# A hybrid HGRN2 and Hyena layer: even and odd filter spectra added by transfers, the filter network's chain kept together, h modulated by ScalarE

## The chip, the core and the metric

The kernel runs on one core of a Trainium2 chip. The core has a matrix engine (TensorE, PE in the profile), a vector engine (VectorE, DVE), a scalar engine (ScalarE, ACT), a general engine (GpSimd, POOL) and a queue engine (SyncE, SP), each with its own in-order stream of instructions, and 16 DMA engines that all queues share. SP, ACT and POOL can issue transfers; the issuing engine's stream stands still while an issue waits for its conditions. The metric is the device time of one execution in microseconds (us). Fast memory on the core is SBUF (128 partitions), PSUM is where PE writes (banks of 128 x 512 f32), DRAM is the chip's main memory.

## The reference, cut to what matters

One layer over 128 context tokens and 512 latent tokens, 640 in all, width 1024: an adaLN modulation, one wide projection, an HGRN2 branch and a Hyena branch, a mix, a norm, a SwiGLU part and a norm. The change touches two things at its start.

The modulation of the input:

```
mod = (silu(cond) @ ada_w + ada_b)        # shift1, scale1, gate1, ...
h = x * (1.0 + scale1) + shift1
proj = h @ w_in
```

And the implicit filters of the long convolution, which depend on weights alone:

```
h = sin(freq[0] * (z @ w1 + b1))
h = sin(freq[1] * (h @ w2 + b2))
h = sin(freq[2] * (h @ w3 + b3))
h = h @ w4                                # 64 -> 2 x 1024 (forward, backward)
h = h.reshape(L, 2, D_B) * window[:, None, :]
kern = concatenate([h_fwd, 0, flip(h_bwd[1:])])
K = rfft(kern, n=2 * L);  U = rfft(u, n=2 * L)
y = irfft(U * K, n=2 * L)[:, :L] + u * skip
```

## The kernel before, in words

The program has one long first stage, in function `start`, and then the projection, the branches and the rest. A plan (`PLAN`, a string of tokens) sets in which order the first stage's steps are written; a scheduler then places every instruction on its engine by what is ready and by that order, so that neighbours on an engine are not always neighbours in the plan.

The steps that the change and the prediction speak of:

- **The filter network** (`filter_mlp`, L493 to L511). Three layers on all 640 positions, two halves of 320 side by side. PE multiplies (L496, L501, L507), then DVE does four steps (add and scale L480, round L482, subtract L483, clamp L484) and ACT the sine (L171). The result goes to `hf_hi`, `hf_lo`, a high and a low part in a rounded f32 format: every large product of this kernel is three products, high by high, high by low and low by high.
- **Filter chunks** `cc` = 0 to 3, 256 of the 1024 channels each. `kern_load` (token L) loads the last weights `w4` and the window `win`; `kern_a` (A) forms sums and differences of the weights on DVE (`wsd`, L535), splits them (`whi`, `whl`), multiplies (`ks`, L544 and L545), multiplies by the window on DVE (`af`, two buffers) and splits again (`abh` by a cast, `abl` by a subtraction on DVE or POOL). An `af` buffer is free when both parts are there. Two `win` buffers exist: the load of window 2 waits for the last `af` of chunk 0, that of window 3 for the last `af` of chunk 1.
- **The chunks' spectra**, `kern_b` (B). With tables `kth`, `ktl`, loaded and split by `ktab` (tokens k0 to k2), PE makes the products `kp` (L573) and `k` (L586): for two groups `kt` an even and an odd part. ACT copies the even part out of PSUM (`ev`), and DVE makes `ko` = odd + even and even - odd (L602, L603, recorded under L182). `kern_store` (W) writes `ko` to the DRAM tensor `kd`, issued by ACT. `kd` is read much later, in `spectrum`, by loads on SP.
- **x and h.** Tokens x and T load a tile of 128 tokens and transpose it on PE (L458), ACT and DVE copy it to `xT`. Tokens D and M load 1 MB pieces of `ada_w` (`araw`, eight pieces in this stage) on SP, multiply them (L407), copy (`md`, L418), transpose (`adaT`, L431) and add into `modT`. Token h (`make_h`, L463) makes h for one of eight groups of 128 columns: a multiply-add in place on `xT` for 128 and 512 tokens, on ACT or on DVE by the string `HMOD` (L469), then a cast to `hTh` and a subtraction to `hTl`.
- **The value projection** (token V). Two units of 120 products (`v`, L715) read h and weights `raw`, loaded on SP (L350) and split into `wh` by ACT (L358) and `wl`. The first products of the next stage are `ma` (L675).

Small helpers record most of these: L182 is every two-operand operation, L185 every copy or cast by a string of engine letters (`COPIES`), L171 every ACT function. PSUM has three banks for `mm` tiles and five that all of `ks`, `kp`, `k` and the x transposes share.

Of the kernel before, what the change touches and what calls it, by code (L numbers as in the profile page):

```python
# [118 lines left out]
PLAN = """x0 k0 L0 k1 x4 k2 p mlp t L1 T0 x3 T4 A0 x2 D0 T2 A1 x1 L2 B0 M0 T1 D2 A2 M2 T3 h0 L3 B1 D1 A3 h1 B2 M1 D3 h2 h3 M3 h4 W2 W0 h5 h6 h7 W1 q V0 e0 B3 g0 W3 V1 m w0 e2 10 20 g1 50 11 60 g2 70 21 30 40 w1 w2 61 51 52 12 71 Q8 62 22 g3 w3 13 41 g4 53 72 Q9 42 31 63 w4 g5 23 14 w5 73 Z4 Q10 43 32 g6 w6 64 24 15 54 74 Q11 33 65 25 44 16 26 55 75 Q12 Z5 g7 34 w7 66 45 56 17 76 Q13 35 67 46 g8 27 57 w8 18 77 Z6 Q14 g9 g10 36 w9 28 19 68 37 29 58 78 Q15 69 47 59 w10 79 Q16 38 110 210 Z7 g11 610 49 111 510 39 48 w11 211 g12 611 112 w12 212 710 Q17 g13 511 711 Q18 410 113 w13 311 612 Z8 310 411 512 712 Q19 513 213 613 412 713 312 413 313 Z9"""  # L119
HMOD = "SVSSVSSS"  # L120
# [43 lines left out]
def body(tc, I, O):  # L164
# [5 lines left out]
    def act(out, in_, func, bias=0.0, scale=1.0):  # L170
        r = S.activation(out, in_, func, bias=bias, scale=scale)  # L171
# [282 lines left out]
    def x_transpose(t, xs):  # L454
        for q in range(2):
            ps = sc_bank(f"xT{t}_{q}")
            for k in range(4):
                PE.transpose(ps[:, k * P:k * P + P], xs[:, (4 * q + k) * P:(4 * q + k + 1) * P], ident)  # L458
# [34 lines left out]
    def filter_mlp():  # L493
# [5 lines left out]
        for hf in range(2):  # L499
            cs = slice(hf * ORD, hf * ORD + ORD)  # L500
            PE.matmul(ps[cs, 0:HT], w2[cs], h1[cs], start=True, stop=True)  # L501
# [98 lines left out]

    def order_after(ins, prev):
        if prev is not None:  # L602
            tc.add_manual_dep(  # L603
                ins.ins, prev.ins.name,
                mybir.DependencyInfo(mybir.DependencyClass.NoSync, mybir.DependencyReason.DATA),
                reason="issue order")
# [123 lines left out]
    def start():  # L730
# [43 lines left out]
        for tok in PLAN.split():  # L774
            if tok == "mlp":
                if HP:
                    with tc.high_priority():
                        filter_mlp()
                else:
                    filter_mlp()  # L780
# [1026 lines left out]
```

## Time and profile before

| | us |
|---|---|
| median of 3 runs | 1414.06 (1412.3 to 1414.61) |
| the profiled execution, its own time | 1413.15 |
| the profiled execution, span from first to last instruction | 1411.4 |
| PE busy | 1371.7 (97%) |
| DVE, ACT, POOL busy | 995.7, 620.0, 63.4 |
| PE busy in the first 150 | 125.56 |
| first `ks` product, first `kp`, first `ma` start at | 23.26, 36.99, 115.52 |

The profile is one execution. A row of a timeline gives start, length, engine, source line, operation, what is written and read, shape, how many, and in brackets how long the engine was idle just before and who ended that. A row of the groups gives busy us and mean ns, and idle time before with its releasers. Neighbouring matmuls overlap, so that a row is longer than the step from its start to the next one's. `SPq` and `ACTq` are rows of issued transfers.

### The profile page before, as it was taken

How to read it: one execution, taken by the hardware profiler on the slowest of the kernel's cores; microseconds unless marked ns; L12 is line 12 of the kernel's file. 1: busy time of each engine (PE TensorE's matmuls, PEld its weight loads, DVE VectorE, ACT ScalarE, POOL GpSimd, SP SyncE). 2: the span in 40 equal slices, each digit the busy share in tenths (PEclk: the TensorE clock that was granted, in tenths of full speed). 3: DMA queues.
4: the chain of work that ended last, by engine and by line, in shares of the span. 5: the costliest groups of instructions: out<-in, count | busy, mean ns of one | idle time of the engine just before them, and what ended most of it. 6: DMA issues, size and time to landing. Idle time of an engine off the chain costs nothing. (4 is left out here: it accounts for less than half of the span.)

```text
span 1411.4 us, 23424 instructions
## 1 busy us (share of the span) xinstructions
PE 1371.7 (97%) x9513; PEld 1290.8 (91%) x9513; DVE 995.7 (71%) x1752; ACT 620.0 (44%) x1010; POOL 63.4 (4%) x56
## 2 busy tenths in 40 slices
PE   4999999999999999999999999999999999999997
PEld 2689889899999999999999999988999999998886
DVE  6886786656889743648888786568987776765426
ACT  3555554442323211536655655227654443542121
POOL 4230000010000000000000000000000000000003
PEclk9999999999999999999999999999999999999999
DMA  7944666675323373432222223551653213267211
GB/s 246 334 139 146 208 207 195 184 232 193 101 83 102 90 246 131 135 115 82 81 86 77 64 63 109 174 196 75 169 162 102 81 59 118 89 201 263 75 60 75
DMA packets 198855, 195.63 MB, mean 139 GB/s; under 512 B 7581, under 2 KB 155773, under 8 KB 197980
## 3 DMA queue, kind: packets, MB, share of 16 engines
q1 hardware_dynamic: 194860, 179.75, 40.5%
q0 software_dynamic: 2160, 9.15, 1.8%
q10 hardware_dynamic: 1728, 5.24, 0.9%
q8 instruction: 74, 1.21, 0.4%
q14 instruction: 33, 0.27, 0.1%
HBM read 162.91 MB, written 31.21 MB: 138 GB/s over the span
## 5 line engine op out<-in xcount | busy, mean ns | idle before, releaser
L182 DVE TENSOR_TENSOR wl<-raw,wh 128x1024 fp32r<-128x1024 f32 x96 | 117.3, 1223 | 133.1 <-ACT wh L358 132.3
L358 ACT CAST wh<-raw 128x1024 fp32r<-128x1024 f32 x90 | 94.1, 1049 | 220.9 <-PE pb L612 41.0
L1431 PE MATMUL fo<-wh,act 128*128 128x512 f32 (+1 forms) x440 | 130.7, 380 | 0.0
L1431 PEld LDWEIGHTS fo<-wh,act 128*128 128x128 f32 x440 | 81.2, 188 | 16.0
L1431 PE MATMUL fo<-wl,act 128*128 128x512 f32 (+1 forms) x220 | 83.4, 379 | 0.0
L612 PE MATMUL hy<-hTh,wh 128*128 128x320 f32 x256 | 79.6, 311 | 0.0
L612 PE MATMUL hy<-hTh,wl 128*128 128x320 f32 x256 | 79.1, 309 | 0.0
L612 PE MATMUL hy<-hTl,wh 128*128 128x320 f32 x256 | 79.1, 309 | 0.0
L612 PE MATMUL f<-hTh,wh 128*128 128x320 f32 x224 | 70.7, 316 | 0.0
L612 PE MATMUL f<-hTl,wh 128*128 128x320 f32 x224 | 69.7, 311 | 0.0
L612 PE MATMUL f<-hTh,wl 128*128 128x320 f32 x224 | 69.2, 309 | 0.0
L182 POOL TENSOR_TENSOR y<-y,gb 128x512 f32<-128x512 f32 x8 | 11.6, 1454 | 888.4 <-ACT y L171 888.1
L1431 PEld LDWEIGHTS fo<-wl,act 128*128 128x128 f32 x220 | 41.3, 188 | 7.9
L612 PEld LDWEIGHTS hy<-hTh,wh 128*128 128x128 f32 x256 | 48.1, 188 | 0.0
L612 PEld LDWEIGHTS hy<-hTl,wh 128*128 128x128 f32 x256 | 48.1, 188 | 0.0
L612 PEld LDWEIGHTS hy<-hTh,wl 128*128 128x128 f32 x256 | 48.0, 188 | 0.0
L171 ACT ACT_TABLE_LOAD x36 | 46.2, 1283 | 1.4 <-PEq L1791 0.7
L715 PE MATMUL v<-wl,hTh 128*128 128x256 f32 x160 | 45.0, 286 | 1.6 <-DVE wl L182 1.6
L715 PE MATMUL v<-wh,hTl 128*128 128x256 f32 x160 | 45.1, 284 | 0.1
L715 PE MATMUL v<-wh,hTh 128*128 128x256 f32 x160 | 44.9, 285 | 0.0
L612 PEld LDWEIGHTS f<-hTl,wh 128*128 128x128 f32 x224 | 42.2, 188 | 0.0
L612 PEld LDWEIGHTS f<-hTh,wh 128*128 128x128 f32 x224 | 42.1, 188 | 0.0
(2293 smaller groups left out, 4699.6 us busy)
## 6 DMA issues: line engine op xcount, KB each, us to landing
raw<-in_w_in SPq DMA_DIRECT2D x52, 512.0 KB, 3.8
araw<-in_ada_w SPq DMA_DIRECT2D x20, 1024.0 KB, 6.5
rm<-in_w_in SPq DMA_DIRECT2D x28, 512.0 KB, 4.6
rp<-in_ffn_w_in SPq DMA_DIRECT2D x24, 512.0 KB, 5.4
raw<-in_ffn_w_out SPq DMA_DIRECT2D x22, 512.0 KB, 4.6
rf<-in_ffn_w_in SPq DMA_DIRECT2D x18, 512.0 KB, 5.2
sd<-my SPq DMA_DIRECT2D x28, 320.0 KB, 2.3
kk<-kd SPq DMA_DIRECT2D x20, 256.0 KB, 2.7
```

What stands on the lines that cost most here:

```text
L171: r = S.activation(out, in_, func, bias=bias, scale=scale)
L182: return (eng or V).tensor_tensor(out=out, in0=a, in1=b, op=op)
L358: (V.tensor_copy if HIE[i] == "V" else S.copy)(hi, raw)
L612: r = PE.matmul(ps[:, 0:HT], w[a][:, k, :], x[b][:, k, c0:c0 + HT], start=k == 0 and i == 0, stop=k == kt - 1 and i == 2)
L715: PE.matmul(ps[:, (t - t0) * 256:(t - t0) * 256 + 256], hT[b][:, k, t * P:t * P + P], w[a][:, k % 4, :], start=k == 0 and i == 0, stop=k = ...
L1431: PE.matmul(ps, x(t, b, k0 + kk), w[a][:, kk, :], start=first and kk == 0 and i == 0, stop=last and kk == nk - 1 and i == 2)
```

## The change

The plan's first tokens, before:

```
x0 k0 L0 k1 x4 k2 p mlp t L1 T0 x3 T4 A0 x2 D0 T2 A1 x1 L2 B0 M0 T1 D2 A2 M2 T3 h0 L3 B1 D1 A3 h1
B2 M1 D3 h2 h3 M3 h4 W2 W0 h5 h6 h7 W1 q V0 e0 B3 g0 W3 V1 m w0 e2 10 20 g1 50 11 60 g2 70 ...
```

And now:

```
x0 L0 x4 p mlp k0 k1 k2 t L1 x3 T4 A0 x2 D0 T2 A1 x1 L2 B0 W0 M0 T1 D2 A2 M2 T3 h0 L3 B1 W1 D1 A3 h1
B2 W2 M1 D3 h2 h3 M3 h4 h5 h6 h7 q V0 e0 B3 W3 g0 V1 m w0 e2 10 20 g1 50 11 60 K0 g2 70 ...
```

K1, K2 and K3 follow between tokens of the next stage. So the tables (k) are loaded after the network's tokens, T0 has moved into the network, each store (W) stands behind its spectrum (B), and K is new. The diff without the plan:

```diff
-HMOD = "SVSSVSSS"
+HMOD = "SSSSSSSS"
...
-COPIES = {... 'k': 'VSS', ...}
+COPIES = {...}
...
+EVB = 2
...
-    kd = dr.tile([4, P, NB, 2, 256], F32, name="kd")
+    kd = [dr.tile([P, NB, 2, 256], F32, name=f"kd{cc}") for cc in range(4)]
+    evd = [dr.tile([P, 2, 2, 256], F32, name=f"evd{cc}") for cc in range(4)]
...
-    skp_all = sp.tile([1, D], F32, name="skp_all")
...
-        G.dma_start(skp_all, I["hy_skip"])
...
-    def x_transpose(t, xs):
+    def x_transpose(t, xs, after=None):
...
+                if q == 0 and k == 0:
+                    order_after(x, after)
...
-        V.tensor_scalar(a, a, HALF, -HALF, ALU.min, ALU.max)
-        act(a, a, AF.Sin, scale=-TWO_PI)
+        net["clamp", nm] = V.tensor_scalar(a, a, HALF, -HALF, ALU.min, ALU.max)
+        net["sin", nm] = act(a, a, AF.Sin, scale=-TWO_PI)
...
-            PE.matmul(ps[cs, 0:HT], w2[cs], h1[cs], start=True, stop=True)
+            net["f2"] = PE.matmul(ps[cs, 0:HT], w2[cs], h1[cs], start=True, stop=True)
         h2 = sin_layer(ps[:, 0:HT], 1, "2")
+        x_transpose(0, xs0, net["f2"])
...
-        cpy("k", i, kth[:, cs], raw)
+        order_after(S.copy(kth[:, cs], raw), net["sin", "2"])
...
-        return w4, win, skp_all[:, c0:c0 + 256]
+        skp = sp.tile([1, 256], F32, tag="skp", bufs=2, name=f"skp{cc}")
+        SY.dma_start(skp, I["hy_skip"][:, c0:c0 + 256])
+        return w4, win, skp
...
-        tt(wsd[:, 0], w4[:, 0], w4[:, 1], ALU.add)
-        tt(wsd[:, 1], w4[:, 0], w4[:, 1], ALU.subtract)
+        for i, op in enumerate((ALU.add, ALU.subtract)):
+            x = tt(wsd[:, i], w4[:, 0], w4[:, 1], op)
+            if cc == 0:
+                order_after(x, net["clamp", "2"])
...
-            ev = sp.tile([P, 2, 256], F32, tag="ev", bufs=1, name=f"ev{cc}_{kt}")
-            cpy("o", 3 * cc + 1 + kt, ev, pk[0].rearrange("p (x n) -> p x n", x=2))
-            od = pk[1].rearrange("p (x n) -> p x n", x=2)
+            ev, od = (x.rearrange("p (x n) -> p x n", x=2) for x in pk)
+            e = sp.tile([P, 2, 256], F32, tag="ev", bufs=EVB, name=f"ev{cc}_{kt}")
+            cpy("o", 3 * cc + 1 + kt, e, ev)
             t = kout(2, kt)
-            tt(t[:, 0], od, ev, ALU.add)
-            tt(t[:, 1], ev, od, ALU.subtract)
-            out.append((t, 2 * kt, 2))
+            S.copy(t[:, 0], od)
+            S.mul(t[:, 1], od, -1.0)
+            out.append((t, 2 * kt, 2, e))
...
-        for t, f, n in out:
-            KQ.dma_start(kd[cc, :, f:f + n], t)
+        for t, f, n, e in out:
+            KQ.dma_start(kd[cc][:, f:f + n], t)
+            if n == 2:
+                KQ.dma_start(evd[cc][:, f // 2], e)
+
+    def kern_add(cc):
+        for kt in range(2):
+            for i in range(2):
+                G.dma_start(kd[cc][:, 2 * kt + i], evd[cc][:, kt], accum_op=ALU.add)
```

`order_after(a, b)` only fixes that `a` stands behind `b` on their engine; it waits for nothing more. The odd part is copied twice by ACT, once with its sign turned, and stored to `kd`; the even part is stored to a DRAM tensor of its own (`evd`); then POOL issues transfers (`kern_add`) that add `evd` into `kd` in DRAM, four for each chunk. An adding transfer waits until both stores it needs have landed.

The network, DVE between its second and third layer. Before (`kth` and `whl` are the table's and the weights' casts, `wsd` the weights' sums):

```order
L484 TENSOR_SCALAR sa_175<-sa_175 128x320
L185 CAST kth<-kt_141 128x768
L182 TENSOR_TENSOR wsd_259<-w_0_145 128x256 x2
L480 TENSOR_SCALAR sa_185<-f_182,fpar 128x320
L482 TENSOR_SCALAR sk_187<-sa_185 128x320
L185 CAST whl_264<-whi_262 64x512
L483 SCALAR_TENSOR_TENSOR sa_185<-sk_187,sa_185 128x320
L182 TENSOR_TENSOR whl_264<-wsd_259,whi_262 64x512
L484 TENSOR_SCALAR sa_185<-sa_185 128x320
```

Now:

```order
L493 TENSOR_SCALAR sa_170<-sa_170 128x320
L489 TENSOR_SCALAR sa_180<-f_177,fpar 128x320
L491 TENSOR_SCALAR sk_182<-sa_180 128x320
L492 SCALAR_TENSOR_TENSOR sa_180<-sk_182,sa_180 128x320
L493 TENSOR_SCALAR sa_180<-sa_180 128x320
L189 TENSOR_TENSOR wsd_268<-w_0_147 128x256 x2
```

The second layer's four steps follow the first layer's with nothing in between; the casts and the sums stand behind them. On ACT, from the first layer's sine to the third's, now (`sa_180` is the second layer's sine, `sa_204` the third's first half, `xT` the copies of two x tiles):

```order
L192 COPY xT_137<-xT_1_194 128x2x128
L171 ACTIVATE sa_180<-sa_180 128x320
L192 COPY xT_138<-xT_1_194 128x2x128
L192 CAST whi_271<-wsd_268 128x512
L527 CAST kth<-kt_224 128x768
L192 COPY xT_135<-xT_0_254 128x2x128
L192 COPY xT_136<-xT_0_254 128x2x128
L527 CAST kth<-kt_228 128x768
L192 COPY xT_137<-xT_1_261 128x2x128
L171 ACTIVATE sa_204<-sa_204 128x320
```

All three casts of the table are ACT's now, and two of them stand ahead of the third layer's sine.

The turn to the value projection. ACT before (`md` is the copy of the last ada product, `wh` the casts of the first `raw` tiles):

```order
L418 COPY md_861<-ada_852 128x512
L599 DMA kd<-ko_1_679 128x1024
L358 CAST wh_919<-raw_917 128x1024
L358 CAST wh_925<-raw_923 128x1024
L358 CAST wh_931<-raw_929 128x1024
L185 CAST abh_0_701<-af_0_697 128x512
```

ACT now, and PE now from the end of chunk 1's products:

```order
L613 DMA kd_67<-ko_1_697 128x1024
L363 CAST wh_938<-raw_936 128x1024
L363 CAST wh_944<-raw_942 128x1024
L423 COPY md_889<-ada_880 128x512
L192 CAST whl_714<-whi_712 64x512
L363 CAST wh_950<-raw_948 128x1024
```

```order
L600 MATMUL k_1_1_670<-abh_4_398,ktl 128x256
L412 MATMUL ada_880<-araw_0_866,scT 32x512 x4
L412 MATMUL ada_880<-araw_1_868,scT 32x512 x4
L436 MATMUL adaT_891<-cst,md_889 128x128 x4
L558 MATMUL ks_0_717<-whl_714,hf_hi 128x512
L559 MATMUL ks_0_717<-whl_714,hf_lo 128x512
```

The copy `md` and chunk 3's `whl` now stand behind two casts of `raw`, and PE's next rows read `md` and `whl`. Before, `ks` of chunk 3 (which stood between the two halves of this ada product) and the products of chunk 2 came before any row that needs `raw`.

POOL's queue now, from the first to the third chunk's `abl` (`kd<-evd` are the adding transfers):

```order
L189 TENSOR_TENSOR abl_1_372<-af_1_367,abh_1_371 128x512
L620 DMA kd_66<-evd_70 128x512 x2
L189 TENSOR_TENSOR abl_3_390<-af_3_387,abh_3_389 128x512
L189 TENSOR_TENSOR abl_4_399<-af_4_396,abh_4_398 128x512
L620 DMA kd_66<-evd_70 128x512 x2
L189 TENSOR_TENSOR abl_0_541<-af_0_536,abh_0_540 128x512
```

Before, the four `abl` rows followed each other.

More of the change, by code (lines that the diff above doesn't have):

```diff
@@ L116, in _constants @@
     return {k: np.ascontiguousarray(v) for k, v in c.items()}
[L119 to L120 removed]
+PLAN = """x0 L0 x4 p mlp k0 k1 k2 t L1 x3 T4 A0 x2 D0 T2 A1 x1 L2 B0 W0 M0 T1 D2 A2 M2 T3 h0 L3 B1 W1 D1 A3 h1 B2 W2 M1 D3 h2 h3 M3 h4 h5 h6 h7 q V0 e0 B3 W3 g0 V1 m w0 e2 10 20 g1 50 11 60 K0 g2 70 21 30 40 w1 w2 61 51 52 12 71 K1 Q8 62 22 g3 w3 13 41 g4 53 72 Q9 K2 42 31 63 w4 g5 23 14 w5 73 Z4 Q10 K3 43 32 g6 w6 64 24 15 54 74 Q11 33 65 25 44 16 26 55 75 Q12 Z5 g7 34 w7 66 45 56 17 76 Q13 35 67 46 g8 27 57 w8 18 77 Z6 Q14 g9 g10 36 w9 28 19 68 37 29 58 78 Q15 69 47 59 w10 79 Q16 38 110 210 Z7 g11 610 49 111 510 39 48 w11 211 g12 611 112 w12 212 710 Q17 g13 511 711 Q18 410 113 w13 311 612 Z8 310 411 512 712 Q19 513 213 613 412 713 312 413 313 Z9"""
+HMOD = "SSSSSSSS"
 HSUB = "GVVVVGVG"
@@ L141 @@
 PSA2 = dict(mm=("mm", 4), sc=("x", 4), o=("x", 4), tr=("x", 4))
-COPIES = {'x': 'SSVSSSSSSS', 'h': 'SSSSSSSV', 'm': 'SV', 'k': 'VSS', 'w': 'SVVS', 'v': 'VSSS', 'a': 'SSSSSSSSSVVSSSSSSSSS', 'o': 'SSSSSSSSVSSS'}
+COPIES = {'x': 'SSVSSSSSSS', 'h': 'SSSSSSSV', 'm': 'SV', 'w': 'SVVS', 'v': 'VSSS', 'a': 'SSSSSSSSSVVSSSSSSSSS', 'o': 'SSSSSSSSVSSS'}
 ASUB = "GVVVGVGVGGGGVGVGVVVG"
 KSUB = "GGG"
-HP = False
+EVB = 2
 PS0 = {'mm': ('mm', 3), 'sc': ('x', 5), 'o': ('x', 5), 'tr': ('x', 5)}
@@ L179, in act, with order_after @@
         return r
+    def order_after(ins, prev):
+        if prev is not None:
+            tc.add_manual_dep(
+                ins.ins, prev.ins.name,
+                mybir.DependencyInfo(mybir.DependencyClass.NoSync, mybir.DependencyReason.DATA),
+                reason="issue order")
     def tt(out, a, b, op, eng=None):
@@ L457, in x_transpose @@
             for k in range(4):
-                PE.transpose(ps[:, k * P:k * P + P], xs[:, (4 * q + k) * P:(4 * q + k + 1) * P], ident)
+                x = PE.transpose(ps[:, k * P:k * P + P], xs[:, (4 * q + k) * P:(4 * q + k + 1) * P], ident)
+                if q == 0 and k == 0:
+                    order_after(x, after)
             for i in range(2):
@@ L475, in make_h @@
         tt(hTl[:, k, :], xT[:, k, :], f32(hTh[:, k, :]), ALU.subtract, G if HSUB[k] == "G" else V)
+    net = {}
     def sin_layer(psrc, i, nm):
@@ L491, in body, with filter_mlp @@
     ktl = sp.tile([P, 2304], F32R, name="ktl")
-    def filter_mlp():
+    def filter_mlp(xs0):
         ps = sc_bank("f1")
@@ L576, in kern_b @@
         cpy("o", 3 * cc, t[:, 0], pk.rearrange("p (x n) -> p x n", x=2))
-        out = [(t, 4, 1)]
+        out = [(t, 4, 1, None)]
         for kt in range(2):
@@ L587, in kern_b @@
                                       start=i == 0 and j2 == 0, stop=i == 2 and j2 == 1)
-            ev = sp.tile([P, 2, 256], F32, tag="ev", bufs=1, name=f"ev{cc}_{kt}")
-            cpy("o", 3 * cc + 1 + kt, ev, pk[0].rearrange("p (x n) -> p x n", x=2))
-            od = pk[1].rearrange("p (x n) -> p x n", x=2)
+            ev, od = (x.rearrange("p (x n) -> p x n", x=2) for x in pk)
+            e = sp.tile([P, 2, 256], F32, tag="ev", bufs=EVB, name=f"ev{cc}_{kt}")
+            cpy("o", 3 * cc + 1 + kt, e, ev)
             t = kout(2, kt)
-            tt(t[:, 0], od, ev, ALU.add)
-            tt(t[:, 1], ev, od, ALU.subtract)
-            out.append((t, 2 * kt, 2))
+            S.copy(t[:, 0], od)
+            S.mul(t[:, 1], od, -1.0)
+            out.append((t, 2 * kt, 2, e))
         return out
     def kern_store(cc, out):
-        for t, f, n in out:
-            KQ.dma_start(kd[cc, :, f:f + n], t)
[L601 to L606, printed above, removed]
+        for t, f, n, e in out:
[6 more added lines that the diff above has]
+                G.dma_start(kd[cc][:, 2 * kt + i], evd[cc][:, kt], accum_op=ALU.add)
     def dense_fm(w, x, half, ps, kt=KT, after=None):
@@ L746, in step @@
                 kern_store(i, ab[i])
+            elif op == "K":
+                kern_add(i)
             elif op == "k":
@@ L775, in start @@
             if tok == "mlp":
[L776 to L780, printed above, removed]
+                filter_mlp(xs[0])
                 continue
@@ L972, in spectrum @@
         kk = q.tile([P, 2, 256], F32, tag="kk", bufs=2, name=f"kk{cc}_{f}")
-        SY.dma_start(kk, kd[cc, :, (0, 2, 1, 3, 4)[f]])
+        SY.dma_start(kk, kd[cc][:, (0, 2, 1, 3, 4)[f]])
         ps = sc_bank(f"fw{cc}_{f}")
```

## The prediction

> **What bounds the kernel now.** I read the windows by stage first, to see where TensorE (PE) is idle at all.
>
> ```profile
> 0.00:150.00 150.00, 125.56 (x854) 105.75 (x855) 114.99 (x213) 77.97 (x140) 39.10 (x37) 0.98 0.65 216
> 150.00:300.00 150.00, 148.73 (x1003) 135.08 (x1002) 105.05 (x174) 75.39 (x131) 2.72 (x1) 1.00 0.66 204
> 300.00:1380.00 1080.00, 1075.61 (x7543) 1031.32 (x7542) 751.72 (x1308) 461.94 (x731) 9.97 (x10) 1.00 0.38 120
> ```
>
> The first number after the length is PE's busy time. It idles 24.4 us in the first 150, 1.3 in the next 150 and 4.4 in the 1080 after. The order of the work differs only in the first 170 us or so, so whatever is won or lost by the first matmul of the stage that follows (`ma`) reaches the end nearly whole. Six rows of PE's timeline come next (start, length, engine, line, operation, and in brackets the idle time ahead of it and who ended that).
>
> ```profile
> 8.57 1.33 PE L501 MATMUL f<-sa,w 64*64 64x320 f32 x4 [2.46 <-ACT sa L171]
> 17.12 1.44 PE L507 MATMUL f<-sa,w 64*128 64x320 f32 x4 [7.22 <-ACT sa L171]
> ...
> 23.26 0.73 PE L544 MATMUL ks<-whl,hf_hi 128*128 128x512 f32 x2 [1.44 <-ACT hf_hi L185]
> ...
> 36.99 0.39 PE L573 MATMUL kp<-abh,kth 128*128 128x256 f32 x1
> ...
> 44.01 0.60 PE L458 MATMUL xT<-cst,xs 128*128 128x128 f32 x4
> ...
> 115.52 0.31 PE L675 MATMUL ma<-hTh,wmg0h 128*128 128x320 f32 x1
> ```
>
> The longest wait is the filter network's third layer (L507). Between its second and third layer stand VectorE (DVE) and ScalarE (ACT) rows that wait for loads:
>
> ```profile
> 10.45 0.56 DVE L185 CAST kth<-kt 128x768 fp32r<-128x768 f32 x1 [2.43 <-DMA kt<-in_kt]
> 12.76 0.76 DVE L182 TENSOR_TENSOR wsd<-w 128x256 f32<-128x256 f32 x2 [1.75 <-DMA w<-in_filt_w]
> 13.44 0.60 DVE L480 TENSOR_SCALAR sa<-f,fpar 128x320 f32<-128x320 f32 x1
> ...
> 15.87 0.83 ACT L185 CAST kth<-kt 128x768 fp32r<-128x768 f32 x1 [1.70 <-DMA kt<-in_kt]
> 16.61 0.47 ACT L171 ACTIVATE sa<-sa 128x320 f32<-128x320 f32 x1
> 19.07 0.83 ACT L185 CAST kth<-kt 128x768 fp32r<-128x768 f32 x1 [2.00 <-DMA kt<-in_kt]
> ```
>
> A second limit runs beside it, the loads on SP's queue. Filter window 3 waits for DVE's last `af` of the chunk before; eight 1 MB loads (`araw`) and the first weights (`raw`) stand behind it.
>
> ```profile
> 46.69 0.55 SPq L527 DMA_DIRECT2D win<-in_win  x1
> 47.36 10.54 SPq L398 DMA_DIRECT2D araw<-in_ada_w  x4
> 57.98 3.62 SPq L350 DMA_DIRECT2D raw<-in_w_in  x3
> ...
> araw<-in_ada_w SPq DMA_DIRECT2D x1, 1024.0 KB, 7.6
> ...
> 32.50:35.00 2.50, 2.50 (x10) 1.83 (x7) 2.01 (x4) 1.22 (x2) 1.15 (x1) 0.53 0.13 37
> 45.00:47.50 2.50, 2.48 (x17) 1.14 (x10) 2.50 (x5) 1.17 (x3) 0.65 (x1) 1.00 0.10 40
> 60.00:70.00 10.00, 10.00 (x70) 6.27 (x65) 7.96 (x20) 7.16 (x12) 2.60 (x2) 1.00 1.07 376
> ...
> 68.38 2.95 ACT L358 CAST wh<-raw 128x1024 fp32r<-128x1024 f32 x3
> ```
>
> In windows the last two numbers are the DMA engines' busy share and GB/s. Outside the two holes at 32.5 and 45 they are full (1.07, 376 GB/s), and just when they have delivered `raw`, ScalarE casts it (68.38) and PE turns to the value projection. So this stage has two clocks that tie, PE and the transfers. A shorter start pays only if the transfers follow. The last 1 MB load is issued by 57.98 - 0.55 = 57.4 (0.55 as the issue above) and lands 7.6 later, at 65.0; two `raw` loads of 0.52 MB at 376 GB/s, 1.4 us each, then make the second `raw` land at about **67.8**. No row gives that landing itself; the second cast's start bounds it at 69.4 (68.38 and one cast of 1.0).
>
> **Part 1, the network's chain.** Layer 2 ends on PE at 8.57 + 1.33 = 9.90. DVE's four steps on it began at 13.44, 3.5 later than they could; now they follow at once. The lengths that this part needs (busy us, mean ns):
>
> ```profile
> L482 DVE TENSOR_SCALAR sk<-sa 128x320 f32<-128x320 f32 x4 | 1.3, 323 | 0.1
> L483 DVE SCALAR_TENSOR_TENSOR sa<-sk,sa 128x320 f32<-128x320 f32 x4 | 2.0, 488 | 0.1
> L185 ACT COPY xT<-xT 128x256 f32<-128x256 f32 x18 | 5.6, 379 | 1.4 <-PE xT L458 1.4
> L185 ACT CAST hf_hi<-sa 128x320 fp32r<-128x320 f32 x1 | 0.5, 461 | 0.0
> L185 ACT CAST hTh<-xT 128x640 fp32r<-128x640 f32 x7 | 5.1, 731 | 2.0 <-DVE xT L469 2.0
> ```
>
> 0.60 + 0.32 + 0.49, and the clamp at 0.33 like the step before: 1.75, so 11.7; the sine (0.47) ends at 12.2 and layer 3 starts there, 4.9 earlier. The eight transposes of x_prompt now ahead of layer 3 lie in the gap; their input landed by 10.45, since it is issued ahead of the kt load that DVE got then. But behind layer 3 ScalarE's order is now kt cast, two copies, kt cast, copy, third sine. The kt loads move behind the first window and one x tile; the last of them still lands near 19.07, as the same bytes are ahead of it, and the second one load earlier (0.39 MB at 376 GB/s, 1.0), at 18.0. Cast 0.83, copy 0.38, sine 0.47, third kt cast 0.83 and the cast of the network's output 0.46 add 3.0: `ks` starts near **21.0**, 2.3 ahead of 23.26. Were ScalarE held by nothing, layer 3's end at 13.7 and two passes of DVE's steps would give 18; were the loads 2 us later than I take them, nothing is gained: -5 to 0. Then the first chunk's chain no longer has four copies of x ahead of its casts on ScalarE, and one ada product moves behind `kp`: I take `kp` at 32.5, 4.5 ahead, and the end of the products behind it at 40.5, 3.5 ahead of 44.01, because ScalarE now empties more of the banks between them.
>
> **Part 2, the adding transfers.** Removed from DVE, added to ScalarE:
>
> ```profile
> L182 DVE TENSOR_TENSOR ko<-k,ev 128x512 f32<-128x512 f32 x8 | 5.5, 682 | 0.1
> L182 DVE TENSOR_TENSOR ko<-ev,k 128x512 f32<-128x512 f32 x8 | 5.4, 678 | 0.0
> L469 DVE TENSOR_SCALAR xT<-xT,modT 128x512 f32<-128x512 f32 x2 | 4.1, 2026 | 0.0
> L185 ACT COPY ev<-k 128x512 f32<-128x512 f32 x7 | 4.1, 589 | 4.7 <-DVE ko L182 3.9 <-PE k L586 0.8
> L171 ACT ACTIVATE xT<-xT,modT 128x512 f32<-128x512 f32 x6 | 4.9, 810 | 0.0
> L171 ACT ACTIVATE xT<-xT,modT 128x128 f32<-128x128 f32 x6 | 3.0, 498 | 0.0
> ```
>
> DVE loses 5.5 + 5.4 + 4.1 = 15.0 us. ScalarE gains 16 x 0.59 = 9.4, and for two modulations 2 x (0.81 + 0.50) = 2.6; with eight more stores to issue, about 15. DVE's relief is off PE's path until `af` of chunk 1, and that is what frees window 3: I take its issue at **43.7**, 3.0 ahead of 46.69 (it follows the 3.5 above).
>
> What the DMA engines get in their place is charged here. Per chunk: two stores of 0.26 MB and four adding transfers of 0.26 MB. No row shows an adding transfer. The nearest rows are the transfers GpSimd issues, and the old stores:
>
> ```profile
> q0 software_dynamic: 2160, 9.15, 1.8%
> ...
> kd<-ko ACTq DMA_DIRECT2D x6, 512.0 KB, 3.7
> ```
>
> 1.8% of 1411.4 us is 25.4 us of all 16 engines for 9.15 MB, 360 GB/s: a copy's rate. I take an adding transfer as one copy, 0.7 us, being nearest to that row; the bounds are 0 (it runs beside loads that do not fill the engines) and 3 copies, 2.1 us (two reads and a write one after the other). The Trainium skill, *DMA: Bandwidth & Descriptors*, "Rules for kernel authors", says that an accumulate reads its destination and writes it later, and that queues share the same 16 engines; by it the estimate is the upper bound, rival B below. No row here shows it either way.
>
> Between window 3's issue and the second `raw`'s landing the old kernel stores 1.3 MB (two parts of 0.52, one of 0.26). Now it is 0.26 + 0.52 of chunk 0, 1.05 of its adding transfers, and 0.52 + 0.52 + 0.26 + about half of the late 0.52: 3.4. That is 2.1 MB more, 5.6 us at 376 GB/s. So the second `raw` lands at 67.8 - 3.0 + 5.6 = **70.4**.
>
> **Part 3, what waits for it.** In the new order ScalarE casts two `raw` tiles, then copies `md`, then `whl`; PE's next matmuls (`adaT`, then `ks` of chunk 3) wait for just these. In the old kernel `md` came before the casts and PE had `ks` and `k` work. So `ks` of chunk 3 starts at 70.4 + 1.0 + 0.6 + 0.6 = 72.6 (a cast, then the md and whl copies, as long as the `ev` copy); PE idles before it some 10 us, which is where its lead is spent. From there to `ma` stand 10 `ks` and 348 products:
>
> ```profile
> 65.08 0.40 PE L544 MATMUL ks<-whl,hf_hi 128*128 128x512 f32 x1
> 65.31 0.39 PE L545 MATMUL ks<-whl,hf_lo 128*128 128x512 f32 x1
> ...
> 101.13 0.28 PE L715 MATMUL v<-wh,hTh 128*128 128x256 f32 x1
> 115.40 0.28 PE L715 MATMUL v<-wl,hTh 128*128 128x256 f32 x1
> ```
>
> 0.23 each, and 120 from 101.13 to 115.52, 0.12 each: 2.3 + 41.8 + 0.2 of transposes = 44.3. `ma` starts at 116.9 for 115.52: **1.4 us later**. The modulations on ScalarE cost nothing in this sum: from there its work to the last h part is seven pairs of 1.3, six casts of 0.73 and some 11 copies of 0.6, about 20 us, to 93, and the 176 products after the last part (21.1) could end at 114.
>
> GpSimd's queue now waits twice per chunk for a store to land (3.7) and then issues; behind it stand the `abl` of the next chunk, for whose slot DVE's next `af` waits. While `k` products are left on PE this is hidden; uncovered it is up to 3.7 a time.
>
> **Sum.** The profiled execution took 1413.15 for a span of 1411.4. With +1.4: 1414.5, against a median of 1414.06, which the profiled one is 0.9 below. About 0.2% (2.8 us) is what a measurement here can tell from no change; so this is no change.
>
> **The rivals.**
> A, *the lead survives* (faster). If the loads fill the two holes (2.2 us each lost at 32.5 and 45) and adding transfers cost the loads nothing, `raw` comes by 65 and PE keeps its lead at `kp`, 4.5 to 6: 1407 to 1409. For: DVE's waits and the holes both hang on the same late chain. Against: 60 to 70 is full already.
> B, *the transfers decide* (slower). At 3 copies each, chunk 0's four add 4 x 1.4 = 5.6 and half of chunk 1's 1 to 2: `raw` at 77.5, `ma` at 124, +8.5: 1421.5. It decides from about 1.5 copies on (+2.8). For: 1.07 busy. Against: queue 0's 360 GB/s.
> C, *ScalarE or GpSimd's queue decides* (slower). ScalarE was busy 7.2 of 10 us from 60 to 70 and gets 15 us more by 110; two uncovered waits of 3.7 on GpSimd's queue, or layer 3 no earlier because of the kt casts (+2.6): +3 to +6, 1416.5 to 1419. For: its order is fixed and holds loads. Against: DVE's 15 us gone.
> That the sums stay on the path (the change does nothing of what it says) I rule out: the 16 DVE rows are gone from the order.
>
> **How the numbers follow.** Forecast 0.42, A 0.30, B 0.18, C 0.10. The forecast's own range, 1411.3 to 1417, is the "same" case. Range 1406.5 to 1418.5: it takes in A, C and half of the way to B. Faster 0.30; same 0.42; slower 0.28.
>
> **What would show it.** Layer 3 at 12 to 13 and `ks` at 20 to 21 show part 1; `kp` at 32 to 33 and window 3 near 44 the lead; an idle PE between 60 and 72 released by `adaT` or `whl`, and `raw` casts waiting for a DMA, show part 3; `ma` near 116.9 shows the sum. A full DMA row up to 77 is B; PE with no gap near 65 and `ma` at 110 is A. I am wrong if PE's gap there is released by GpSimd or VectorE, or if `ma` moves and the end does not.

## The result

The changed kernel takes 1429.40 us (median of 4 runs, 1428.70 to 1430.36) against 1413.29 for the kernel before: a ratio of 1.0118, 95% interval 1.0105 to 1.0130. It is 16 us slower, where no change had been forecast. The profiled execution took 1429.06 us for a span of 1427.2.

PE's windows of the changed kernel by stage (start and end, length, busy us of PE, PEld, DVE, ACT and POOL, granted clock, DMA share, GB/s):

```profile
0.00:150.00 150.00, 115.89 (x743) 97.47 (x744) 98.33 (x180) 82.27 (x149) 51.63 (x52) 0.87 0.82 239
150.00:300.00 150.00, 148.78 (x1003) 135.28 (x1002) 105.15 (x168) 76.22 (x134) 0.00 (x0) 1.00 0.63 195
300.00:1380.00 1080.00, 1075.66 (x7571) 1032.43 (x7570) 757.48 (x1323) 464.93 (x738) 12.78 (x11) 1.00 0.39 124
```

Nearly all of it lies in the first 150 us: PE is busy 115.89 there for 125.56, and 111 matmuls fewer are done. Over the whole span PE idles 48.7 us for 39.7 and is busy 1378.5 for 1371.7, so 9.0 us are idle time and 6.8 are the same work done more slowly: the mean clock of the stage is 0.87 for 0.98.

PE's timeline of the changed kernel at the places that the prediction spoke of (start and us, then the idle time ahead and what ended it):

```profile
12.71 0.88 PE L517 MATMUL f<-sa,w 64*128 64x320 f32 x4 [0.83 <-ACT sa L171]
20.57 1.22 PE L558 MATMUL ks<-whl,hf_hi 128*128 128x512 f32 x2 [3.50 <-ACT hf_hi L192]
30.98 0.77 PE L558 MATMUL ks<-whl,hf_hi 128*128 128x512 f32 x1 [2.85 <-DVE whl L189]
36.85 0.39 PE L587 MATMUL kp<-abh,kth 128*128 128x256 f32 x1
54.79 0.66 PE L463 MATMUL xT<-cst,xs 128*128 128x128 f32 x4 [2.22 <-DVE af L189]
67.62 1.94 PE L412 MATMUL ada<-araw,scT 128*32 128x512 f32 x8 [3.61 <-DMA araw<-in_ada_w]
79.01 0.66 PE L436 MATMUL adaT<-cst,md 128*128 128x128 f32 x4 [3.24 <-ACT md L423]
89.09 0.58 PE L600 MATMUL k<-abh,kth 128*128 128x256 f32 x1 [4.39 <-ACT ko_p L192]
```

The group of the first `ma` (min/median/max ns of one, first and last start):

```profile
L689 PE MATMUL ma<-hTh,wmg0h x4: 309/309/312, 133.4 to 134.7; 128*128 128x320 f32 x4
```

The network's third layer starts 4.4 us earlier than before and `ks` 2.7, but `kp` no earlier (36.85 for 36.99). From there PE falls behind in the four waits of the last rows, for VectorE, for a load and twice for ScalarE, and `ma` starts 17.9 us late. VectorE's timeline of the same execution:

```profile
21.85 2.05 DVE L189 TENSOR_TENSOR wsd<-w 128x256 f32<-128x256 f32 x1
24.22 0.67 DVE L189 TENSOR_TENSOR af<-ks,win 128x512 f32<-128x512 f32 x1
82.08 5.75 DVE L565 SCALAR_TENSOR_TENSOR af<-af,skp 1x256 f32<-1x256 f32 x1
```

ScalarE's, at the second cast of `raw` and ahead of PE's last wait:

```profile
77.42 1.04 ACT L363 CAST wh<-raw 128x1024 fp32r<-128x1024 f32 x1 [0.39 <-DMA raw<-in_w_in]
87.94 0.62 ACT L192 CAST abh<-af 128x512 fp32r<-128x512 f32 x1 [2.74 <-DVE af L565]
```

GpSimd's:

```profile
17.19 6.42 POOL L189 TENSOR_TENSOR ktl<-kt,kth 128x768 fp32r<-128x768 f32 x3 [8.30 <-ACT kth L527]
50.95 1.78 POOL L620 DMA_DIRECT2D kd<-evd  x2 [5.05 <-issue]
81.72 2.68 POOL L189 TENSOR_TENSOR wl<-raw,wh 128x1024 fp32r<-128x1024 f32 x1
84.64 2.90 POOL L189 TENSOR_TENSOR wl<-raw,wh 128x1024 fp32r<-128x1024 f32 x1
```

SP's waits (us in total, times, longest):

```profile
SPq L403 <- DMA kd<-ko_p: 8.1, 1, 8.1
```

SP's issues at that place (timelines), two 1 MB loads in one row before, and the second of the same two now:

```profile
33.76 1.17 SPq L398 DMA_DIRECT2D araw<-in_ada_w  x2
42.52 0.37 SPq L403 DMA_DIRECT2D araw<-in_ada_w  x1
```

The DMA queues' part of the page (packets, MB, share of 16 engines' span):

```profile
q0 software_dynamic: 4432, 13.34, 3.7%
```

Four things to read there. VectorE has rows several times their length (2.05 us for the 0.41 of the same row at 26.57, 5.75 for the 0.41 at 88.83) just while GpSimd has rows of its own. GpSimd stands still for 5.05 us ahead of the first adding transfers; the row names no releaser (`issue`), the rows of later ones name a store `kd<-ko`. SP's queue waits 8.1 us, ahead of a 1 MB `araw` load, for a store of the kind `kd<-ko_p` to land; before, no row of SP's waits names a store to `kd`. And queue 0 takes 3.7% of 1427.2, 52.8 us of all 16 engines, for 1.8% of 1411.4, 25.4: sixteen adding transfers are 27.4 us, **1.71 each** (the shares are rounded to 0.1%, so 1.6 to 1.8).

### The profile page after: what moved, and what is told of

It is laid out like the page before. It is cut to its first block, busy times and chain, and to the rows that moved or that the text cites. A ratio compares the mean times of both kernels' runs of the same rounds, so it can differ in the third digit from the quotient of the medians.

```text
span 1427.2 us, 23471 instructions
## 1 busy us (share of the span) xinstructions
PE 1378.5 (97%) x9513; PEld 1297.9 (91%) x9513; DVE 987.8 (69%) x1731; ACT 631.6 (44%) x1031; POOL 76.0 (5%) x71
## 3 DMA queue, kind: packets, MB, share of 16 engines
q10 hardware_dynamic: 2880, 7.34, 1.3%
```

## The experiments

Each kernel ran beside the kernel before on the same chip; the ratio's 95% interval stands in brackets, and microseconds are (ratio - 1) x 1413. The diffs of e1 to e3 show only what differs in kind. e5, e10 and e14 leave the even part out of the spectra, e6 the odd part, and e12 the tables' low part.

| run | what it is | ratio | us |
|---|---|---|---|
| (the change) | | 1.0118 [1.0105, 1.0130] | +16.7 |
| e4 | h on ScalarE alone | 0.9993 [0.9984, 1.0003] | -1.0 |
| e2 | network order alone | 1.0042 [1.0027, 1.0057] | +5.9 |
| e1 | both, sums on VectorE | 1.0042 [1.0027, 1.0057] | +5.9 |
| e3 | sums by transfers alone | 1.0148 [1.0131, 1.0165] | +20.9 |
| e10 | e3 without adding transfers | 1.0059 [1.0041, 1.0078] | +8.3 |
| e5 | change without adding transfers | 1.0052 [1.0037, 1.0067] | +7.3 |
| e6 | change, plain copies for adding | 1.0085 [1.0070, 1.0100] | +12.0 |
| e7 | change, adding in one go at 130 us | 1.0171 [1.0156, 1.0186] | +24.2 |
| e11 | change, adding one by one, 130 to 300 us | 1.0145 [1.0125, 1.0166] | +20.5 |
| e8 | change, first wl on VectorE | 1.0130 [1.0115, 1.0145] | +18.4 |
| e9 | e2, chunk 2's whl early | 1.0010 [1.0001, 1.0019] | +1.4 |
| e12 | e2, no ktl | 1.0025 [1.0015, 1.0035] | +3.5 |
| e13 | change, md and whl first | 1.0151 [1.0135, 1.0166] | +21.3 |
| e14 | e5, md and whl first | 1.0067 [1.0054, 1.0081] | +9.5 |
| e15 | e9, h on ScalarE, tables early | 1.0015 [1.0006, 1.0024] | +2.1 |
| e16 | e9, h on ScalarE, ktl on VectorE | 0.9984 [0.9975, 0.9993] | -2.3 |
| e17 | e4, ktl on VectorE | 1.0018 [1.0009, 1.0027] | +2.5 |
| e18 | change with e16's two mends | 1.0128 [1.0112, 1.0143] | +18.1 |

### The three parts apart: e1, e2, e3, e4

The first theory (T) put it all on the adding transfers, its rival (N) on the network's order.

e1 is the change with

```diff
-            S.copy(t[:, 0], od)
-            S.mul(t[:, 1], od, -1.0)
-            out.append((t, 2 * kt, 2, e))
+            tt(t[:, 0], od, ev, ALU.add)
+            tt(t[:, 1], ev, od, ALU.subtract)
```

without `evd` and `kern_add`, and the stores at their old tokens.

> The change without its adding transfers: VectorE makes the even and odd sums again, the network's chain and h on ScalarE stay. Theory T (the adding transfers cost the time: each holds the 16 DMA engines 1.7 us, 27.4 us for 16 by queue 0's row, and GpSimd stands still before each pair): 1408 to 1414, ma at 110 to 115, no PE gap released by araw near 65. Theory N (the network's new order costs it: PE at half clock from 16 to 35 us, so the lead of 2.7 us at the first ks is gone at kp): 1420 or more, ma at 122 or later. If only the lead is lost and nothing else, 1413 to 1415.

e2 is e1 with the old `HMOD`:

```diff
-HMOD = "SSSSSSSS"
+HMOD = "SVSSVSSS"
```

> The network's new order alone (sums on VectorE, old split of h). If the network order is what costs the 5.4 us that stayed without adding transfers (1418.6): 1417 to 1420, with PE at half clock between 20 and 35 us and a PE gap near 50 behind VectorE. If h on ScalarE is what costs it: 1410 to 1414.

e3 is the change with the old network order and the old `HMOD`:

```diff
-        x_transpose(0, xs0, net["f2"])
-                order_after(x, net["clamp", "2"])
-        order_after(S.copy(kth[:, cs], raw), net["sin", "2"])
+        cpy("k", i, kth[:, cs], raw)
```

> The adding transfers alone on the old network order and the old split of h between VectorE and ScalarE (the skip vector in four small loads, as the change has it, since the second ev buffer needs the room). Theory T: 1426 to 1431, as slow as the whole change, with PE gaps released by araw and by a GpSimd abl. Theory N: 1413 to 1416, since the old order keeps PE's clock.

e4 is the kernel before with

```diff
-HMOD = "SVSSVSSS"
+HMOD = "SSSSSSSS"
```

> h's modulation on ScalarE alone, on the kernel before. If it costs the 5.4 us: 1417 to 1420. By the prediction it is free: 1412.5 to 1414.

h on ScalarE is free (e4), as predicted. The network's order, meant as a gain, costs 5.9 us by itself (e2, and e1 the same). The sums by transfers cost 20.9 by themselves (e3). Neither theory is whole: both parts cost, and they do not add up (26.8 apart, 16.7 together). The sums by transfers are here all that comes with them, the copies on ScalarE and the moved and additional stores too.

### Why the network's order costs: e9, e12

Behind its start, e2's PE waits longest here (its timeline):

```profile
51.19 0.77 PE L557 MATMUL ks<-whl,hf_hi 128*128 128x512 f32 x1 [4.43 <-DVE whl L189]
```

VectorE's timeline of e2 has these rows ahead of that `whl`:

```profile
47.24 0.68 DVE L189 TENSOR_TENSOR ko<-k,ev 128x512 f32<-128x512 f32 x1
47.84 1.22 DVE L192 CAST abh<-af 128x512 fp32r<-128x512 f32 x1
48.97 0.68 DVE L189 TENSOR_TENSOR ko<-ev,k 128x512 f32<-128x512 f32 x1
49.57 0.74 DVE L192 COPY xT<-xT 128x256 f32<-128x256 f32 x2
50.33 0.72 DVE L189 TENSOR_TENSOR whl<-wsd,whi 64x512 fp32r<-64x512 f32 x1
```

In the kernel before, the same `whl` stood at 43.06, ahead of the second pair of `ko` sums. e9 puts it there again:

```diff
-        cpy("w", cc, whi, wsd)
-        cpy("v", cc, whl[0:ORD], f32(whi[0:ORD]))
-        tt(whl[ORD:P], wsd[ORD:P], f32(whi[ORD:P]), ALU.subtract)
+        with (tc.high_priority() if cc == 2 else ExitStack()):
+            cpy("w", cc, whi, wsd)
+            cpy("v", cc, whl[0:ORD], f32(whi[0:ORD]))
+            tt(whl[ORD:P], wsd[ORD:P], f32(whi[ORD:P]), ALU.subtract)
```

> The network's order alone, with the cast and the subtraction that make chunk 2's whi and whl put three places earlier on VectorE, ahead of the second pair of ko sums; nothing else there moves by more than a place. Theory O (the new order costs 5.5 us because scheduling put chunk 2's whl behind these sums and two copies, so that PE waits 4.4 us at 51 and then runs its ks at half clock): 1413 to 1416, kp of chunk 1 near 54 for 58.9. Theory L (it costs because the network's lead is lost before the first kp): unchanged, 1418 to 1420.

Chunk 1's `kp` starts at 54.11 for 58.91, and the cost falls from 5.9 to 1.4 us: 4.5 us of it went with one row of VectorE's order, which the scheduler had moved when the network's rows moved. Not all of this is shown to be that row's: in the profiled executions the first `kp`, ahead of it, already comes at 35.43 for 36.53, and PE's granted clock from 20 to 35 us is 1.00 in e9 and 0.50 in e2, though nothing that the edit names lies there.

e12 takes GpSimd's three table rows out of e2:

```diff
     ktl = sp.tile([P, 2304], F32R, name="ktl")
+    G.memset(ktl.bitcast(F32), 0.0)
...
-        tt(ktl[:, cs], raw, f32(kth[:, cs]), ALU.subtract, G if KSUB[i] == "G" else V)
```

> The network's order alone, with the table's low part (ktl) set to zero ahead of everything in place of GpSimd's three subtractions (so K lacks its smallest products). If GpSimd's rows at 17 to 23.6 us hold up VectorE there (its rows of 2.0 to 2.2 us for 0.4 to 0.7) and with it eat the network's lead: no VectorE row over 1 us from 17 to 25, first af at 22 to 23 for 24.2, first kp at 34 to 35 for 36.5, and 1415 to 1418. If PE's half clock eats it: first kp at 36 to 37, 1418 to 1420.

VectorE's rows of e12 at the place where e2 and the change have the 2 us rows:

```profile
21.25 0.41 DVE L189 TENSOR_TENSOR wsd<-w 128x256 f32<-128x256 f32 x1
21.58 0.48 DVE L189 TENSOR_TENSOR hf_lo<-sa,hf_hi 64x320 fp32r<-64x320 f32 x1
22.30 0.69 DVE L189 TENSOR_TENSOR af<-ks,win 128x512 f32<-128x512 f32 x1 [0.25 <-PE ks L558]
```

`wsd` is 0.41 again, the first `af` starts at 22.30 for 23.88, the first `kp` at 34.1 for 36.5, `ma` at 117.8 for 120.3, and the time falls by 2.4 us (the two intervals overlap). So GpSimd's rows took a good part of the network's lead: the change moves the tables, and with them these rows, to 17 to 23.6 us, where VectorE needs the network's last steps. In the kernel before two of the three had ended by 18.6. How much is less sure: these are single executions, and e3 and e10, which differ in nothing up to there, have their first `kp` 1.6 us apart (34.78 and 36.38). That PE ran its first `ks` at about half its pace in the change (1.22 for two, 0.73 before) has a part that no run took apart: PE's clock from 20 to 40 us was 0.91 in e12 and 0.60 in e2; but e4, which loses nothing, had 1.22 there too.

That a lead at `ks` need not reach `kp` is shown by more than the change: in it and in e5, e6, e7, e8, e11, e13 and e14, whose edits all lie behind `kp`, the first `ks` starts anywhere from 19.54 to 23.75 and the first `kp` always from 36.35 to 37.85.

### What the adding transfers cost, and where: e5, e6, e7, e11, e10

e5 and e10 empty `kern_add` in the change and in e3:

```diff
-        for kt in range(2):
-            for i in range(2):
-                G.dma_start(kd[cc][:, 2 * kt + i], evd[cc][:, kt], accum_op=ALU.add)
+        pass
```

> The change with the sixteen adding transfers left out (so the even part is missing from K), all stores and ScalarE copies kept. Theory T: 1408 to 1414. If ScalarE's 15 us of extra work and the eight more stores cost the time instead: 1424 or more. Theory N: 1424 or more.

> The old network order with ScalarE's copies and all stores, without the sixteen adding transfers (so the even part is missing from K). If the adding transfers are all of the 19.9 us that they cost on the old order: 1412 to 1415. If the eight more stores and ScalarE's copies have a part in it: 1416 or more. Below 1411: moving the sums off VectorE is worth something if adding is free.

e6 copies in place of adding:

```diff
-                G.dma_start(kd[cc][:, 2 * kt + i], evd[cc][:, kt], accum_op=ALU.add)
+                G.dma_start(kd[cc][:, 2 * kt + i], evd[cc][:, kt])
```

> The change with the sixteen adding transfers turned into plain copies of the same bytes from the same place to the same place, with the same waits (so K's products hold the even part alone). If the adding itself is dear (1.7 us of the 16 engines by queue 0's row, against 0.7 for a copy): a good half of the 9.5 us that the adding transfers cost comes back, 1422 to 1425, and queue 0 takes 11 us less. If GpSimd's standing still and the DRAM traffic as such cost it: 1428 to 1430.

The sixteen adding transfers cost 9.3 us on the new order (16.7 - 7.3) and 12.6 on the old (20.9 - 8.3). Queue 0's row of e6:

```profile
q0 software_dynamic: 3408, 13.34, 2.6%
```

2.6% of e6's span of 1424.0 is 37.0 us, less 25.4: 0.73 for a copy of 0.26 MB, so adding takes **2.35 times** as long on the same engines (2.1 to 2.7 with the rounding of the shares). That dearness is half of the cost: 4.7 of the 9.3 us go with it, and as plain copies they still cost 4.7.

e7 and e11 move them out of the stage:

```diff
+        if "late" not in net:
+            net["late"] = G.tensor_copy(net["v"][0:1, 4, 0:1], net["v"][0:1, 4, 0:1])
...
+                order_after(G.dma_start(...), net["late"])
```

> The change with all sixteen adding transfers behind the second value unit's store (a one-element copy on GpSimd that waits for it), at about 130 us, where GpSimd has nothing to do until 300. Theory T, with the place deciding (in the first stage they hold up araw and raw, later nothing is near its limit: DMA share 0.63 from 150 to 300): the same as without them, within 2 us. If their engine time costs wherever it stands: 1420 to 1429.

```diff
                 SY.dma_start(sd[slot[kind, t]], dst)
+                add_one(dst)
```

Here `add_one` copies one element of `dst` on GpSimd and issues the next of the sixteen behind that.

> The change with the sixteen adding transfers one by one, each behind another finished tile of the next stage (about one in 10 us from 150 to 310, by a one-element copy on GpSimd). If an adding transfer costs only what it holds up, and a single one of 1.7 us between loads holds up nothing there (DMA share 0.63): 1418 to 1421, as without them. If each delays a load that PE waits for: 1428 or more.

Both expected the place to decide; both were wrong by far. PE's longest wait in e7, from its timeline:

```profile
151.51 0.64 PE L691 MATMUL ma<-m4h,wma0h 128*128 128x320 f32 x1 [15.41 <-ACT mu L700]
```

What that `mu` stood behind on ScalarE (its timeline; `wma1h` is a cast of the next stage's weights `rm`):

```profile
150.52 0.62 ACT L636 CAST wma1h<-rm 128x512 fp32r<-128x512 f32 x1 [17.67 <-DMA rm<-in_w_in]
```

The window around it (columns as above):

```profile
140.00:160.00 20.00, 8.49 (x44) 8.19 (x45) 6.94 (x11) 4.97 (x9) 4.87 (x6) 0.61 1.03 206
```

The longest wait of PE that is new in e11:

```profile
185.55 0.41 PE L697 MATMUL ma<-m4h,wma3h 128*128 128x320 f32 x1 [4.07 <-ACT mu L706]
```

In one go they fill the DMA engines (share 1.03 at only 206 GB/s) while the next stage's weights wait, and PE stands still for 15.4 us. (In e7 queue 0's share is 3.4% of 1435.2, which makes an adding transfer 1.46 us there.) One by one, between loads that leave a third of the engines idle on average (a share of 0.63 in the row of the change for 150 to 300 us), they still cost 13.1 us more than leaving them out, 0.8 each; the `mu` of the 4.07 us too stands behind a weight cast of ScalarE's that had waited for `rm` (3.73 us). No place that was tried had room for them.

### What is left without adding: e13, e14

e10 is 8.3 us slower than the kernel before although VectorE is busy 8.7 us less (987.0 for 995.7) and nothing is added. Its PE waits for loads (timeline):

```profile
49.38 1.07 PE L412 MATMUL ada<-araw,scT 128*32 128x512 f32 x8 [1.75 <-DMA araw<-in_ada_w]
68.57 1.06 PE L412 MATMUL ada<-araw,scT 128*32 128x512 f32 x8 [3.48 <-DMA araw<-in_ada_w]
74.76 1.12 PE L436 MATMUL adaT<-cst,md 128*128 128x128 f32 x4 [5.12 <-ACT md L423]
```

Its SP's waits have this row:

```profile
SPq L403 <- DMA kd<-ko_p: 8.4, 1, 8.4
```

It is the wait of the change again: SP's fourth 1 MB `araw` of the stage waits for the first store to land, and goes out at 43.1 us (42.5 in the change) for about 34.6 before. The store itself goes out no earlier than before (38.48 in the change, 38.62 before), so what changed is its place in the plan. That alone does not make the wait either: e18 below has the same place and issues both loads from 35.60 on without it, and e9 and e15, with the stores at their old places, have one of 7.5 and 8.9 us for `kd<-ko` at a later load. Why a load waits for a store there no run shows. Whether the last wait, ScalarE's `md` behind two casts that wait for `raw`, is what costs was part 3 of the prediction. e13 (the change) and e14 (e5) put `md` and chunk 3's `whl` first:

```diff
+            for first in ada.get("first", ()) if i < 4 else ():
+                order_after(r, first)
```

where `r` is the weight cast and `first` holds the copy `md` and ScalarE's cast of `whl`. PE's timeline of e14 at the places of the gap follows the two expectations.

> The change with ScalarE's copy md and cast whl of chunk 3 ahead of the first two weight casts; nothing else of ScalarE's order there moves. If these two rows behind casts that wait for raw cost PE's gap of 3.2 us at 79 and what follows: adaT at 75 to 76 for 79.0, 1423 to 1427. If PE's work behind them waits for raw just as long: the gap moves to the first v, 1428 to 1430.

> The same without the sixteen adding transfers (the even part missing from K). Against 1.0052 of the kernel before for the change without them: 1.000 to 1.002 if the order of these two rows is the cost (PE's gap of 5.6 us at 75 closed to below 2), 1.004 or more if it is not.

```profile
69.34 0.66 PE L440 MATMUL adaT<-cst,md 128*128 128x128 f32 x4 [0.71 <-ACT md L425]
77.66 0.38 PE L606 MATMUL k<-abh,kth 128*128 128x256 f32 x1 [2.37 <-ACT ko_p L192]
95.02 0.39 PE L733 MATMUL v<-wh,hTl 128*128 128x256 f32 x1 [0.87 <-POOL hTl L189]
97.35 0.54 PE L733 MATMUL v<-wh,hTl 128*128 128x256 f32 x1 [1.00 <-DVE hTl L189]
```

In e14 the gap closes to 0.71, chunk 3's `ks` starts at 69.85 for 75.70 in e5, and `ma` only at 121.8 for 122.8: most of the 5.9 us are spent again in waits for `ko_p` and `hTl` (4.2 in the three rows), and the time does not fall (1.0067, the intervals overlap). e13 is slower than the change; an `araw` wait of 5.15 us at 52.9, which the change does not have, came with it, so it settles nothing. The gap is real and worth about 1 us at `ma`, and nothing that the time shows. Of e10's 8.3 us, the store that SP waits for and the 2.1 MB more of stores (queue 10: 7.34 MB for 5.24) are the candidates that the rows show; no run took them apart, and this stays open.

### GpSimd in VectorE's way: e8, e16, e17

e8 takes the first two `wl` rows off GpSimd:

```diff
-WSUB = "VGGVVGGG"
+WSUB = "VVVVVGGG"
```

> The change with the first two weight subtractions (wl) moved from GpSimd to VectorE. If VectorE's 5.75 us row at 82 us stood still for GpSimd's two wl rows: no VectorE row over 2.5 us there, PE's gap of 4.4 us near 85 gone or below 1.5, 1423 to 1427. If that row was held by something else: the gap stays, 1429 to 1432 with VectorE's 2.4 us more.

VectorE's timeline of e8 at the row that took 5.75 us in the change:

```profile
85.71 0.40 DVE L565 SCALAR_TENSOR_TENSOR af<-af,skp 1x256 f32<-1x256 f32 x1
```

The row of 5.75 us is 0.40, and VectorE's rows beside four adding transfers that GpSimd issues from 80.69 to 84.91 have their usual lengths (0.68 for an `af` at 84.06): its arithmetic was the block, not its issuing. PE's gap near 85 is gone, yet the time is no better. The profiled execution, the slowest of the four, has an `araw` wait of 7.96 us at 66.6, ahead of the edit, for 3.61 in the change; whether that is what took the gain back no run shows.

e15 and e16 are attempts at a version that keeps the lead: e9 with h on ScalarE, and the tables loaded at their old place (e15) or late with

```diff
-KSUB = "GGG"
+KSUB = "VVV"
```

> The network's chain kept together and T0 in it, chunk 2's whl early, h on ScalarE, sums on VectorE, and the tables loaded and cast at their old place, so that GpSimd's first two table rows end before VectorE's third layer. If the lead can be kept so: first af at 21 to 23, first kp at 33 to 35, 0.995 to 0.999 of the kernel before. If it is eaten further on in any case: 0.999 to 1.003.

> The same with the tables late, as the change has them, and their three subtractions on VectorE, so that GpSimd holds it up nowhere before 27 us but VectorE has 3 us more to do. If GpSimd's rows cost more than their work: first af at 23 to 24, 0.998 to 1.001. If VectorE's work is the limit there: 1.002 to 1.005.

e16 is the one version that beats the kernel before, by 0.16% (0.07 to 0.25). Its first `af` came at 25.70, not earlier as expected, but two follow at once; `kp` starts at 35.2, chunk 1's at 52.07, `ma` at 112.8 for 115.52. e15 keeps 2 us rows on VectorE at 16.8 and 21.2 and gains nothing.

e17 has the last edit and h on ScalarE without the network's new order:

> The kernel before with h on ScalarE and the table's three subtractions on VectorE, the network's order as it was. If the network's chain kept together is what gained in e16 (0.9984): 0.999 to 1.001 here. If taking GpSimd's rows off is what gained: 0.997 to 0.9985. If VectorE's 3 us more between the network's layers delay it: above 1.001.

At 1.0018 it is slower than the kernel before, so e16's gain is not the table rows alone: against e17 it is 0.34%. (e17 has a PE wait of 5.31 us at 91 for a `wl` of GpSimd, which may be a matter of its order.) But e17 is a kernel made worse; against e4, h on ScalarE alone (0.9993), e16 is 0.09% faster and the intervals overlap. So with its two costs mended the network's order no longer loses; that it gains is not shown. e18 is the whole change with both mends:

> The whole change with both mends (chunk 2's whl early, the table's subtractions on VectorE). If the costs add up, the network's 5.5 to 7 us come off 1.0118: 1.006 to 1.008. If the adding transfers take the place of what was mended, as the loads decide: 1.010 to 1.013.

1.0128: nothing came back. On the mended order the sums by transfers cost 1.44% (e18 over e16), 20 us, as much as on the old order. In the change the network's costs do not add to those of the transfers. One row of e18's VectorE, beside GpSimd's two `wl`, shows what can take a mended wait's place; such a row takes 0.81 in the change (at 88.09), and PE then waits 2.32 us for the `af` behind it:

```profile
81.08 5.82 DVE L189 TENSOR_TENSOR hTl<-xT,hTh 128x640 fp32r<-128x640 f32 x1 [1.80 <-ACT hTh L192]
```

## Why the prediction was wrong, by its own steps

**Part 1, the layers: right.** Third layer at 12.71 (12.2 predicted), `ks` at 20.57 (21.0), ScalarE's kt casts ahead of the third sine as read from its order.

**Part 1, "I take kp at 32.5, 4.5 ahead": this step failed first.** `kp` came at 36.85, 0.1 ahead. The lead was carried from ScalarE's order to PE without asking who else uses the time in between. VectorE's first `af` came at 24.22 for 24.31: the moved tables put GpSimd's subtractions on top of its rows. The prediction counted the casts of the tables as moved, not the subtractions behind them. e12 prices that at 2.4 us of the 4.5, by one execution of each; for the rest there are the half pace of PE's `ks` (0.43 apart from 31.5 to 35.4, 0.23 in e9) and the spread of single executions, and no run takes these apart. Window 3 was issued at 48.40, not 43.7.

**Part 2, "an adding transfer as one copy": too low.** It is about 2.35 copies, 1.71 us for the 0.7 of the sum, within the bounds of 0 to 3 and nearer to the upper one. The row it was taken from (queue 0's plain loads) is not near to an addition. The Trainium skill, *DMA: Bandwidth & Descriptors*, "Rules for kernel authors", which the prediction set against that row, had the better of it: an accumulate reads its destination and writes later, and e6's 0.73 against 1.71 agrees. The second `raw` had landed for its cast at 77.42; the sum had 70.4, rival B 77.5. B's agreement is in part luck: it took 3 copies and nothing else, while in e5, without any adding, the cast is already 4 us late.

**Part 2, the stores: a wait left out.** The stores were counted in MB only. That a load on SP's queue would wait 8.1 us for one of them to land was not in the sum. In e5, without any adding, the second cast is already at 73.35 for 69.4 at the latest before; how much of these 4 us is that wait and how much the additional stores is open.

**Part 3: the place right, its weight wrong.** PE's gap ahead of `adaT` and `ks` is there and is released by `md`, as said; `ks` of chunk 3 starts at 79.52 for 72.6. But e14 shows that this gap covers other waits: closing it is worth 1 us at `ma`.

**The sum behind it: 44.3 us from `ks` to `ma` became 53.9.** Of these 9.6 us, 4.39 are PE's wait at 89, 2.3 the 23 `k` products behind it, which take 5.1 us where 0.12 apiece would make 2.8, and 2.3 two later waits, for `hTl` (0.77) and `wl` (1.54). The wait at 89 is VectorE's row of 5.75 us: ScalarE's `abh` at 87.94 waited for it, and `ko_p`, for which PE waited, stands right behind that `abh`. The sum had no term for it.

**GpSimd's queue, "While `k` products are left on PE this is hidden": not hidden once.** 5.05 us of standing still at 46 held up `abl`, with it `af`, and PE for 2.8 us (2.22 at 54.8 and 0.56 at 56.0).

Right were h on ScalarE (e4), the place where time is won or lost (nearly all before 150 us), and that `ma`'s shift reaches the end nearly whole (17.9 there, 15.8 in the span). Rival B, the transfers decide, had the mechanism of the larger part (9.3 of the 16.7 us go when the adding is left out, e5) and was nearer to the price of a transfer; its 1421.5 kept the lead and lacked SP's wait and VectorE's blocked rows. What the forecast called "no change" was a lead of 4.5 us that did not arrive, set against 5.6 us of additional transfers where the whole change cost 16.7.

## What to carry to other kernels

A lead at one engine is worth what the next engine can start earlier: follow it to the first row that consumes it, and look for rows of other engines that the same edit moves into that time. An operation handed to transfers is not free just because the DMA engines are partly idle on average; price it in time of all 16 engines (adding here took two to three copies), and ask of every queue what its issues wait for. When a scheduler orders the rows, an edit also moves rows it does not name: compare the whole order of each engine, since 4.5 us went here with one subtraction that the edit had moved and not named.
